# Running sums of a background stream, pinned in program order on VectorE

## The chip, the core and the metric

One Trainium2 chip; the kernel is one program on one of its cores. TensorE (PE in the profile) multiplies matrices, VectorE (DVE) and ScalarE (ACT) work element by element, SyncE (SP) issues nearly all transfers from HBM to the on-chip memory. Each engine takes its own instructions in order and waits on semaphores for the others. The metric is the device time of one execution in microseconds; several runs are given by their median.

## The reference

Two layers of a decoder on 512 tokens of width 2048, float32, batch 1. Each layer is modulated by a condition `c`: shift, scale and gate come from `silu(c) @ w_mod[l] + b_mod[l]`, where `c` is one row, so this is a product of a vector with a matrix.

```python
def reference(x, c, w_mod, ...):
    c_act = jax.nn.silu(c)
    for l in range(DEPTH):                                  # DEPTH = 2
        mod = c_act @ w_mod[l] + b_mod[l]                   # 2048 -> 3 x 2048
        shift, scale, gate = jnp.split(mod, 3, axis=-1)
        h = x * (1.0 + scale[:, None]) + shift[:, None]
        if l < N_A:                                         # layer 0: differential attention, 8 heads
            y = diff_attention(h, a_w_in[l], a_w_out[l], ...)
        else:                                               # layer 1: forgetting attention, 16 heads
            if kv is None:
                kv = shared_kv(x, c_act, kv_w_mod, kv_b_mod, kv_w, kv_b_f)
            y = forgetting_attention(h, b_w_in[l - N_A], b_w_out[l - N_A], *kv)
        x = layer_norm(DN_ALPHA * x + gate[:, None] * y, ln_g[l], ln_b[l])
    return x
```

`shared_kv` has a modulation of its own, `c_act @ kv_w_mod + kv_b_mod` (2048 to 2 x 2048). So six rows of 2048, each a product with a matrix of 2048 x 2048, are needed after the first layer's shift and scale: the gate of layer 0, shift and scale for the shared keys and values, and shift, scale and gate of layer 1.

## The kernel before

**Products.** Every float32 operand is split in a high and a low part (`split`, lines 167 to 169; for weights `WeightStream.step`, lines 93 and 94: ScalarE copies `whi`, VectorE subtracts to get `wlo`). Three matmuls (L173, L174, L175) then make one product. Weights come through `WeightStream`: four staging tiles `wst` filled by SP (L46), three pairs of `whi` and `wlo`. One split covers 256 rows of a weight block of 512 columns and feeds 24 matmuls of 512 columns in a group of four accumulator banks.

**Groups.** `group(job, ...)` runs one block of 512 columns: eight splits, and for each split a burst of six matmuls into each of four PSUM banks, 192 matmuls in all. After each burst it calls `tick`, which takes one step from the list `pieces` (attention steps of the head before: `score`, `turn`, `values`, `store`, evacuations) and up to `bg` steps from the generator `background`. In the last split the `evac` function of the group empties each bank as it ends; the next group reuses the banks.

**Order of work.** A hand-written start (string `START`) computes the first layer's shift and scale and the first products. Then come the groups `kk`, q-k of head 2, v-gate of head 2, then q-k and v-gate of heads 3 to 7, with the attention of the head before in `pieces`. Then four groups of layer 0's output projection (`out_projection`, f = 0 to 3), in the first of which the attention of head 7 runs. Then the shared values and keys (`vj`, `kj`), then layer 1.

**The background stream.** `mod_stream` computes the later modulation rows. For each segment of 512 columns it goes through the 16 row blocks of the matrix: the block is loaded by SP (L368) into `ms`, and VectorE adds it, times the condition's column, to the running sum `macc` (L389 for the first block, L391 for the others). After the last block of a segment `mod_row` splits `macc` (`mhi` on ScalarE, `mlo` on VectorE), sums it over partitions by two matmuls with ones (L411, L412), adds the bias on VectorE (`mrow`, L413) and stores 2 KB (L414). Each sum ends with a `yield`, so one tick with `bg` 1 is one sum. There are two streams:

- The first, 16 segments, 256 sums, in layer 0. An `ms` tile holds two row blocks (512 KB) and there are two such tiles. Ticks take a step only in the q-k groups of heads 3 to 7 (`bg=lambda k: k % 3 > 0`), in the v-gate groups (`k % 4 > 0`) and in the first group of the output projection (`bg` 1). The evacuation of that group's first bank calls `open_n`, which drains what is left of the stream and then folds the shared modulation into columns (`fold`, a transpose at L934).
- The second, 8 segments, 128 sums, in the groups of the shared values and keys; its blocks are single (256 KB), the first 64 in `msk` tiles, the others in `ms`.

**Who sets the order on an engine.** The program is recorded in the order of the Python code, and a scheduler then orders each engine's instructions: by default it may issue an instruction ahead of earlier-written ones if its operands seem ready sooner. Only the start (`tc.manual_schedule`, VectorE) and single instructions pinned by `tc.keep_in_program_order` (one line of `residual_b`) are held. That call records an ordering edge without a wait from the instruction before it on the same engine, so the pinned one isn't issued ahead of that one. Instructions written later may still be issued ahead of it.

Of the kernel before, what the change touches and what calls it, by code (L numbers as in the profile page):

```python
# [13 lines left out]
ALU = mybir.AluOpType  # L14
# [95 lines left out]
def tile_yoco(  # L110
# [24 lines left out]
    V, S, PE, G = nc.vector, nc.scalar, nc.tensor, nc.gpsimd  # L135
# [19 lines left out]
    def acc_bank(name="acc"):  # L155
        return ps.tile([P, 512], F32, name=name, tag="acc", bufs=4)
# [45 lines left out]
    cact = const.tile([P, KT], F32, name="cact")  # L202
# [152 lines left out]
    def mod_stream(segs, new_stage, new_acc, nk, deep=0, new_deep=None):  # L355

        todo = [(i, r) for i in range(len(segs)) for r in range(KT // nk)]
        loaded = {}  # L360
        summed = []

        def load(k):
            i, r = todo[k]
            src, col, _ = segs[i]
            t = new_deep() if k < deep else new_stage()
            rows = src[nk * r * P : nk * (r + 1) * P, col : col + 512]
            nc.sync.dma_start(t, rows.rearrange("(k p) n -> p k n", p=P) if nk > 1 else rows)  # L368
            loaded[k] = t

        def load_upto(k):
            n = len(loads)
            while n < len(todo) and n <= (k + 7 if n < deep else k + 2 // nk):
                load(n)
                loads.append(n)
                n += 1

        loads = []
        load_upto(-1)
        for k, (i, r) in enumerate(todo):  # L380
            load_upto(k)
            if r == 0:
                acc = new_acc()
            t = loaded.pop(k)
            for kk in range(nk):
                kt = nk * r + kk
                w = t[:, kk, :] if nk > 1 else t
                if kt == 0:
                    V.tensor_scalar(acc, w, cact[:, 0:1], None, op0=ALU.mult)  # L389
                else:  # L390
                    V.scalar_tensor_tensor(acc, w, cact[:, kt : kt + 1], acc, op0=ALU.mult, op1=ALU.add)  # L391
                if kt == KT - 1:
                    summed.append(segs[i][2](acc))
                if kt in (1, 5) and summed:
                    if next(summed[0], None) is None:
                        summed.pop()
                yield
        for _ in summed[0]:
            yield
# [22 lines left out]
    with tc.tile_pool(name="start", bufs=2, reuse_waits="tile") as sp, tc.manual_schedule(engines={ET.DVE}):  # L422
# [110 lines left out]
        acc = {}  # L533
# [101 lines left out]
    for dst, src, col, bias, one in (  # L635
# [5 lines left out]
        for f0 in range(0, D, 512):  # L641
            cs = slice(col + f0, col + f0 + 512)
            segs.append((src, col + f0, mod_row(ap, ones_a, dst[:, f0 : f0 + 512], bias[cs], one)))
    background = mod_stream(
        segs,
        lambda: ap.tile([P, 2, 512], F32, name="ms", tag="ms", bufs=2),
# [424 lines left out]
    acc = [acc_bank() for _ in range(TB)]  # L1071
    held = {}
    for i, (half, s) in enumerate(lag):
# [8 lines left out]
        for b in (2 * half, 2 * half + 1):  # L1082
            bs = slice(b * P, (b + 1) * P)
            for kq in range(2):
                kt = 2 * s + kq
# [10 lines left out]
    for dst, col, one in ((mod_dram[1][1:2, :], D, 1.0), (gate_dram[1], 2 * D, 0.0)):  # L1096
        for f0 in range(0, D, 512):
            cs = slice(col + f0, col + f0 + 512)
            segs.append((w_mod[1], col + f0, mod_row(npool, ones_b, dst[:, f0 : f0 + 512], b_mod[1, cs], one)))
    background = mod_stream(  # L1100
        segs,
        lambda: npool.tile([P, 512], F32, name="ms", tag="ms", bufs=3),
# [243 lines left out]
```

## Time and profile before

| what | us |
|---|---|
| median of 3 runs | 2009.19 |
| lowest and highest | 2004.58, 2010.02 |
| the profiled execution | 2010.56 |
| its span, first to last instruction | 2008.7 |
| running sums L389 and L391, VectorE, 384 in all | 281.0 |
| weight splits L94, VectorE, 338 | 403.4 |
| VectorE idle ahead of sums, for their loads | 98.8 |
| SP waiting to issue an `ms` or `msk` load until a sum is done | 143.9 |

The profile gives, for each engine, busy time, share and number of instructions; for each group of instructions line, operation and tiles, and which other engine or transfer ended the wait before it. A line number is one of the kernel as printed above. A matmul of 512 columns is shown with 0.39 us but the next one starts 0.23 us later, since they are pipelined; so a share of 98% for TensorE means that it hardly ever waits, not that it does nothing else. Time that an engine waits matters only where TensorE waits for it in turn.

### The profile page before, as it was taken

How to read it: one execution, taken by the hardware profiler on the slowest of the kernel's cores; microseconds unless marked ns; L12 is line 12 of the kernel's file. 1: busy time of each engine (PE TensorE's matmuls, PEld its weight loads, DVE VectorE, ACT ScalarE, POOL GpSimd, SP SyncE). 2: the span in 40 equal slices, each digit the busy share in tenths (PEclk: the TensorE clock that was granted, in tenths of full speed). 3: DMA queues.
4: the chain of work that ended last, by engine and by line, in shares of the span. 5: the costliest groups of instructions: out<-in, count | busy, mean ns of one | idle time of the engine just before them, and what ended most of it. 6: DMA issues, size and time to landing. Idle time of an engine off the chain costs nothing.

```text
span 2008.7 us, 25012 instructions
## 1 busy us (share of the span) xinstructions
PE 1964.6 (98%) x9115; PEld 1627.1 (81%) x9115; DVE 1335.3 (66%) x2436; ACT 725.6 (36%) x1235; POOL 2.2 (0%) x10
## 2 busy tenths in 40 slices
PE   5999999999999999999999999999999999999996
PEld 4888878888888888788888888888888888888885
DVE  6887865677777777853576666635455555576578
ACT  2432445333333334431263222224343434353232
POOL 0000000000000000000000000000000000000000
PEclk8999999999999999999999999999999999999998
DMA  9994742375757676452346787634323232333664
GB/s 338 348 314 147 237 157 78 111 228 182 226 182 229 191 223 209 161 166 95 118 144 223 234 275 260 224 95 131 100 90 105 95 105 90 104 123 104 215 210 178
DMA packets 263095, 353.79 MB, mean 176 GB/s; under 512 B 18022, under 2 KB 162556, under 8 KB 262204
## 3 DMA queue, kind: packets, MB, share of 16 engines
q1 hardware_dynamic: 260592, 347.99, 53.2%
q10 hardware_dynamic: 2380, 4.21, 0.6%
q8 instruction: 71, 1.16, 0.2%
q14 instruction: 52, 0.43, 0.1%
HBM read 339.47 MB, written 12.66 MB: 175 GB/s over the span
## 4 chain that ended last, share of the span: by engine, by line
PE 87%; DVE 6%; DMA 4%; issue 1%; SPq 1%; ACT 0%; DVEq 0%; ACTq 0%
PE acc L173 25%; PE acc L174 25%; PE acc L175 25%; DMA ms<-in_w_mod_dram 3%; PE sc L173 2%; PE sc L174 2%; PE sc L175 2%; DVE wlo L94 1%; PE o L175 1%; PE o L173 1%; PE o L174 1%; DVE macc L391 1%; PE tr L1203 1%; DMA sms<-in_w_mod_dram 1%; SPq L454 0%
## 5 line engine op out<-in xcount | busy, mean ns | idle before, releaser
L94 DVE TENSOR_TENSOR wlo<-wst,whi 128x1024 fp32r<-128x1024 f32 (+2 forms) x338 | 403.4, 1196 | 278.9 <-ACT whi L93 276.9
L93 ACT CAST whi<-wst 128x1024 fp32r<-128x1024 f32 (+2 forms) x338 | 348.5, 1032 | 640.8 <-PE acc L175 327.5
L173 PE MATMUL acc<-whi,hh 128*128 128x512 f32 x1244 | 488.6, 396 | 1.7 <-DVE sg L680 1.7
L174 PE MATMUL acc<-wlo,hh 128*128 128x512 f32 x1244 | 485.3, 390 | 0.8 <-DVE wlo L94 0.8
L175 PE MATMUL acc<-whi,hl 128*128 128x512 f32 x1244 | 485.0, 390 | 0.0
L173 PE MATMUL acc<-hh,whi 128*128 128x512 f32 x1184 | 470.4, 397 | 0.9 <-DVE part L561 0.5
L174 PE MATMUL acc<-hl,whi 128*128 128x512 f32 x1184 | 462.3, 390 | 0.0
L175 PE MATMUL acc<-hh,wlo 128*128 128x512 f32 x1184 | 462.2, 390 | 0.0
L391 DVE SCALAR_TENSOR_TENSOR macc<-ms,cact,macc 128x512 f32<-128x512 f32 x300 | 224.9, 750 | 86.1 <-DMA ms<-in_w_mod_dram 59.4
L173 PEld LDWEIGHTS acc<-whi,hh 128*128 128x128 f32 x1244 | 234.9, 189 | 49.0 <-PE acc L175 1.4
L175 PEld LDWEIGHTS acc<-whi,hl 128*128 128x128 f32 x1244 | 233.6, 188 | 50.0
L174 PEld LDWEIGHTS acc<-wlo,hh 128*128 128x128 f32 x1244 | 233.8, 188 | 46.7 <-DVE wlo L94 1.2
L175 PEld LDWEIGHTS acc<-hh,wlo 128*128 128x128 f32 x1184 | 222.3, 188 | 48.6
L173 PEld LDWEIGHTS acc<-hh,whi 128*128 128x128 f32 x1184 | 222.6, 188 | 43.5 <-issue 0.9
L174 PEld LDWEIGHTS acc<-hl,whi 128*128 128x128 f32 x1184 | 222.8, 188 | 39.3
L481 DVE SCALAR_TENSOR_TENSOR sacc<-sms,cact,sacc 128x512 f32<-128x512 f32 (+1 forms) x127 | 89.5, 705 | 6.1 <-DMA sms<-in_w_mod_dram 2.4
L710 ACT ACTIVATE e<-e,mn 128x128 f32<-128x128 f32 (+3 forms) x64 | 36.1, 564 | 126.4 <-DVE mn L706 126.2
L1192 ACT ACTIVATE eb<-eb,mnb 128x128 f32<-128x128 f32 (+1 forms) x64 | 36.1, 564 | 95.5 <-DVE mnb L1189 94.4
L1189 DVE CUSTOM_DVE_ANT_0 eb<-sc,biasb 128x128 f32<-128x128 f32 (+1 forms) x64 | 31.4, 490 | 55.4 <-PE sc L175 55.4
L391 DVE SCALAR_TENSOR_TENSOR macc<-msk,cact,macc 128x512 f32<-128x512 f32 x60 | 44.5, 749 | 14.7 <-DMA msk<-in_w_mod_dram 13.6
L1207 DVE TENSOR_TENSOR pTl<-tr,pTh 128x128 fp32r<-128x128 f32 (+1 forms) x64 | 31.2, 487 | 25.2 <-ACT pTh L1206 24.7
L706 DVE CUSTOM_DVE_ANT_0 e<-sc,bias 128x128 f32<-128x128 f32 (+3 forms) x64 | 31.1, 486 | 20.9 <-PE sc L175 20.9
(259 smaller groups left out, 1776.5 us busy)
## 6 DMA issues: line engine op xcount, KB each, us to landing
wst<-in_a_w_in_dram SPq DMA_DIRECT2D x240, 256.0 KB
ms<-in_w_mod_dram SPq DMA_DIRECT2D x64, 512.0 KB
ms<-in_kv_w_mod_dram SPq DMA_DIRECT2D x64, 512.0 KB
wst<-in_kv_w_dram SPq DMA_DIRECT2D x64, 512.0 KB
wst<-in_b_w_in_dram SPq DMA_DIRECT2D x128, 256.0 KB
sms<-in_w_mod_dram SPq DMA_DIRECT2D x56, 512.0 KB
wst<-in_b_w_out_dram SPq DMA_DIRECT2D x48, 512.0 KB
wst<-in_a_w_out_dram SPq DMA_DIRECT2D x32, 512.0 KB
```

What stands on the lines that cost most here:

```text
L93: self.nc.scalar.copy(hi[:, :, :w], st[:, :, :w])
L94: self.nc.vector.tensor_tensor(lo[:, :, :w], st[:, :, :w], hi[:, :, :w].bitcast(F32), op=ALU.subtract)
L173: PE.matmul(dst, lhs[0], rhs[0], start=start, stop=False)
L174: PE.matmul(dst, lhs[0], rhs[1], start=False, stop=False)
L175: PE.matmul(dst, lhs[1], rhs[0], start=False, stop=stop)
L391: V.scalar_tensor_tensor(acc, w, cact[:, kt : kt + 1], acc, op0=ALU.mult, op1=ALU.add)
L481: V.scalar_tensor_tensor(acc, w, sc, acc, op0=ALU.mult, op1=ALU.add)
L706: V.tensor_tensor_reduce(out=e[:, :w], in0=sc[:, :w], in1=st["bias"][:, (3 - i) * P :], scale=-1.0, scalar=3.0e38, op0=ALU.add, op1=ALU.mi ...
L710: S.activation(e[:, :w], e[:, :w], AF.Exp, bias=mn, scale=-1.0, accum_out=rs)
L1189: V.tensor_tensor_reduce(out=e[:, :w], in0=sc[:, :w], in1=bias[:, :w], scale=-1.0, scalar=3.0e38, op0=ALU.add, op1=ALU.min, accum_out=mn)
L1192: S.activation(e[:, :w], e[:, :w], AF.Exp, bias=mn, scale=-1.0, accum_out=rs)
L1207: V.tensor_tensor(pTl[:, 0 : i + 1, ts], src, pTh[:, 0 : i + 1, ts].bitcast(F32), op=ALU.subtract)
```

## The change

```diff
             for kk in range(nk):
                 kt = nk * r + kk
                 w = t[:, kk, :] if nk > 1 else t
+
                 if kt == 0:
-                    V.tensor_scalar(acc, w, cact[:, 0:1], None, op0=ALU.mult)
+                    ins = V.tensor_scalar(acc, w, cact[:, 0:1], None, op0=ALU.mult)
                 else:
-                    V.scalar_tensor_tensor(acc, w, cact[:, kt : kt + 1], acc, op0=ALU.mult, op1=ALU.add)
+                    ins = V.scalar_tensor_tensor(acc, w, cact[:, kt : kt + 1], acc, op0=ALU.mult, op1=ALU.add)
+                tc.keep_in_program_order(ins)
                 if kt == KT - 1:
                     summed.append(segs[i][2](acc))
                 if kt in (1, 5) and summed:
```

Each of the 384 running sums is pinned behind the VectorE instruction that was written just before it. The same instructions run, with the same operands; buffers, loads and ticks are the same. What differs is the place of the sums in VectorE's order, and, where the scheduler follows, the places of the loads on SP and of some matmuls. The numbers of lines behind the change go up by two, so L389, L391, L411, L413 and L934 of the kernel before are L390, L392, L413, L415 and L936 of the changed one.

## Prediction

> **What bounds the kernel now.** I read the shares of busy time first, then TensorE's waits from 180 to 1000 us, then VectorE's work by stage, and last the stretch in which the moved work lands.
>
> ```profile
> PE 1964.6 (98%) x9115; PEld 1627.1 (81%) x9115; DVE 1335.3 (66%) x2436; ACT 725.6 (36%) x1235; POOL 2.2 (0%) x10
> ...
> PE tr L774 <- DVE og L760: 2.7, 3, 1.3
> PE acc L173 <- DVE sg L680: 2.0, 3, 1.0
> PE o L175 <- DVE al L169: 0.6, 1, 0.6
> PE acc L173 <- DVE part L561: 0.5, 1, 0.5
> ```
>
> TensorE is the bound: it idles 44 us of 2008.7. Some 21 us of that lie before 50 us and 17 after the last matmul, and the diff touches neither. Between 180 and 1000 us it idles some 6 us, always for VectorE. So the change can save a few microseconds at most, and it can lose as many as it makes TensorE wait.
>
> ```profile
> 180.00:300.00 120.00, 116.64 (x543) 95.67 (x542) 90.80 (x190) 47.62 (x100) 0.00 (x0) 1.00 0.61 196
> 300.00:400.00 100.00, 99.50 (x484) 82.82 (x483) 59.26 (x149) 45.84 (x98) 0.00 (x0) 1.00 0.29 92
> 400.00:850.00 450.00, 447.95 (x2101) 371.92 (x2100) 343.33 (x679) 167.01 (x330) 0.00 (x0) 1.00 0.65 205
> 850.00:900.00 50.00, 50.00 (x238) 41.15 (x238) 31.23 (x72) 18.71 (x37) 0.00 (x0) 1.00 0.50 156
> ...
> 180.00:280.00 100.00, 34.36 (x47) 0.62 (x1) 1.00 0.66 212
> 280.00:380.00 100.00, 0.28 (x1) 0.00 (x0) 1.00 0.27 87
> 380.00:830.00 450.00, 157.69 (x217) 8.08 (x13) 1.00 0.65 206
> 830.00:900.00 70.00, 4.71 (x7) 1.24 (x2) 1.00 0.46 145
> ```
>
> The first four rows are busy times of PE, PEld, DVE, ACT and POOL, then clock, DMA share and GB/s. The last four are VectorE and ScalarE on the tile `macc` alone. The scheduler has floated 48 running sums (with their splits 47 rows by 280 us) in front of the place where the loop writes them, into 180 to 300 us. There VectorE is busy 91 of 120 us and TensorE misses 3.4 us. The other side is calm: at 850 to 900 us the sums are over, VectorE has 19 us to spare, and TensorE misses nothing.
>
> **What the change moves.** No instruction is added or removed: 384 sums, 512 KB `ms` and 256 KB `msk` loads, 24 rows. I count in weight splits (`wlo`, L94, numbered from 0; four a pair of banks, one per 24 matmuls), because they stand in both programs in the same order. Before: sum 48 lies ahead of split 51, sum 256 (the last of the first stream) ahead of split 139. After: the first sum stands ahead of split 56, the 227th ahead of split 139, the 256th ahead of split 147. This is the loop's own count: 21 ticks in a q-k group and 24 in a v-gate group, 45 a head, 225 in five heads, and the rest in the first group of the output projection.
>
> (1) The early stretch, 180 to 300 us. 48 sums leave (36 us of VectorE at 0.750 us, row L391) and with them 24 loads. TensorE's waits there are 0.5 (`part`), 0.6 (`al`) and 2.2 (`og` at 258 and 275 us), together 3.3 us. Each waits for a chain on VectorE that has sums in it or just ahead. Bounds: 0 if the chains alone are that long, 3.4 (all idle time) if not. I take -3.3, since VectorE falls from 91 to some 55 us of 120 here.
>
> (2) The heads, 330 to 835 us. Sums per head stay the same (before 217 `macc` rows from 380 to 830, splits among them; after 45 a head), only more even: 3, 3, 1, 3 instead of 4, 4, 5, 0. TensorE missed 2 us here, in two evacuations (L680) that keep their sums. 0, from -2 to +3.
>
> (3) The first projection group, 838 to 885 us. It holds the last head's attention and now 29 more sums. Split 139 begins at 838.01 and ends at 839.24; this is where the stretch ends:
>
> ```profile
> 880.93 0.39 PE L411 MATMUL tr<-mhi,ones_a 128*128 128x512 f32 x1
> ...
> 882.87 0.24 PE L934 MATMUL tr<-ident,mrow 32*128 32x32 f32 x1
> ...
> 881.99 0.67 DVE L413 SCALAR_TENSOR_TENSOR mrow<-tr,mrow 1x512 f32<-1x512 f32 x1
> ...
> 883.53 1.28 DVE L899 TENSOR_TENSOR ztmp<-acc,gate 128x512 f32<-128x512 f32 x2
> ...
> 839.24:861.15 21.91, 21.91 (x110) 18.36 (x110) 14.78 (x45) 9.77 (x22) 0.00 (x0) 1.00 0.21 73
> 861.15:883.53 22.38, 22.38 (x110) 18.25 (x109) 10.49 (x27) 9.43 (x20) 0.00 (x0) 1.00 0.58 190
> ```
>
> VectorE does 14.8 + 10.5 = 25.3 us of work in 44.3 us before it evacuates bank 0 (`ztmp`). The 29 sums add 28 x 0.750 + 0.486 = 21.5 us: 46.8 us of work in 44.3. Now the waits. VectorE is in order, a sum waits for its load, and `ms` has two buffers of two sums. The densest run of sums in this trace is the measure:
>
> ```profile
> 710.64 1.54 DVE L391 SCALAR_TENSOR_TENSOR macc<-ms,cact,macc 128x512 f32<-128x512 f32 x2 [1.28 <-DMA ms<-in_w_mod_dram]
> 713.99 1.54 DVE L391 SCALAR_TENSOR_TENSOR macc<-ms,cact,macc 128x512 f32<-128x512 f32 x2 [1.80 <-DMA ms<-in_w_mod_dram]
> ...
> 725.40 1.54 DVE L391 SCALAR_TENSOR_TENSOR macc<-ms,cact,macc 128x512 f32<-128x512 f32 x2 [0.88 <-DMA ms<-in_w_mod_dram]
> ```
>
> From 705.38 to 726.94 it does 14 sums, 1.54 us a sum, while its only other work is four splits; the chain of waits shows 5.6, 3.7 and 4.4 us per load. Splits 140 to 142 get 11 of the sums: 14.8 + 8.2 - 0.7 (an `mlo` that comes later) = 22.3 us of work, against 21.9 us of time, of which 7.1 were waits for scores, exponents and copies. I keep half of these: 26 us, plus 1.5 us for the 1.6 us more work in splits 128 to 139, ends split 142 near 866.7 instead of 861.15. Splits 143 to 147 get the other 18: at 1.54 us, 27.7 us. Their work fits inside: 13.2 for the sums, 4.9 for four splits, 0.7 each for `mlo`, `mrow` and `al`, 2.8 for a norm chain, 1.4 for two `hl`, 24.4 us. So the last sum ends near 894.4, and with ScalarE's copy and the `mlo` (0.6 + 0.7 us, rows L168 and L169) the pair for L411 is ready at 895.8.
>
> What is late next: in the changed program L411, L412 and L934 stand behind all 192 matmuls of the group instead of 18 and 12 earlier, directly ahead of the next group, which begins at 885.21 now. TensorE is in order and waits there. From L411 to the end of the first `ztmp` it now takes 2.9 us without the interposed matmuls; then banks 2 and 3 come 0.9 us late, because six operations of 0.6 us stand between the pairs of evacuations and two bursts last 2.7. Next group: 895.8 + 2.9 + 0.9 = 899.6, against 885.2: +14.4, say +14. The waits inside the attention (L727 and L774, whose inputs come some 2 to 5 us late) are part of these 14, not beside them. Lower bound, no wait at all: 839.2 + 22.3 + 24.4 + 1.3 + 2.9 - 885.2 = +5. Upper, all waits of before kept and loads at 5.6 us throughout: 2.5 at the start, 29.5 and 32 us: +23. The lead of the splits (three buffers, some 11 us) hides none of this, since `ztmp`, L411 and the transposes have no such lead. What follows is light (1.2 us a split of 5.4), so nothing more is lost, and nothing is won back, since TensorE is full.
>
> (4) SP: `ms` loads leave the queue between 180 and 300 us and stand among the weight loads at 840 to 890: 15 loads or 7.9 MB in some 58 us, 136 GB/s more on the 128 there, which is near the 238 GB/s of 704 to 727 us. 0, in the bounds of (3).
>
> (5) The second stream, 128 sums: before in splits 182 to 217, after in 182 to 229, 2 to 3 a split. The fullest splits hold 5.9 us of work for 5.4 us of matmuls, twice, with light ones around. 0; without their lead, +1.
>
> Sum: -3.3 + 14 = +10.7. The profiled execution took 2010.56, the median is 2009.19; on the median, **2020**.
>
> **A rule against it.** The clock is the column before the last two:
>
> ```profile
> 1996.00:1997.00 1.00, 0.00 (x0) 0.95 0.00 0
> 1997.00:1998.00 1.00, 0.00 (x0) 0.50 0.00 0
> ```
>
> The last matmul ends at 1992.6 and the granted clock falls to 0.50 at 1996.9, 4.3 us later; at the start it is 0.50 for 3.1 us of matmuls from 34.26. So a single wait of over 4.3 us at L411 costs half of 3.1, 1.5 us, more. My walk has waits of some 5 us in the attention and 6 to 8 us at L411. [...]
>
> **Rivals.**
> - *The cover holds* (not slower). Place: splits 139 to 147. If scores and loads are early and TensorE's own spare 4 us (`og` ends at 857, L774 is at 861) and the split's lead take up the lateness, only (1) is left: 2005.9. It decides if VectorE's lateness at the first `ztmp` stays under 1.7 us (885.2 - 883.5). For it: loads cost the heads only 41 us over 112 pairs, 0.37 us a pair. Against: the work alone is 2.5 us too much.
> - *Clock gate*, as above, on top: 2021.5.
> - *Heads*: sums pinned among attention steps wait for loads, and a quarter of those 41 us now shows: 2030. Against: the same rate cost 2 us before.
> - *Even or no effect*: gain and loss at their low bounds cancel, or the order hardly matters: 2009. Against: the built order does move, by up to 48 sums.
>
> **Numbers.** Forecast 0.52 (own range 2012 to 2029), clock gate 0.15, cover holds 0.13, heads 0.10, even 0.10. What can be told from no change is 0.3%, 6 us: below 2003.2 or above 2015.2. Faster: half of cover holds, 0.06. Same: the other half, even, and 0.06 of the forecast's low end, 0.23. Slower 0.71. Range 2006 to 2032: down to the cover, up past heads.
>
> **What would show it.** Right: TensorE full from 200 to 300 us; `macc` absent before 320 us and 29 sums between 840 and 900; a wait of several us at L411 (now L413) for `mlo`; the group after it some 10 us later than the early gain alone would put it. Wrong: no TensorE wait from 840 to 900 us, waits on VectorE spread through the heads, or the early waits still there without sums.

## Result, and the profile after

The changed kernel takes 2023.08 us (median of 5 runs, 2021.46 to 2026.01), the kernel before 2007.38 us (median of 5, 2004.58 to 2010.02): 1.0077 times as long, 95% interval 1.0066 to 1.0088, some 15.7 us more (the two profiled executions took 2023.51 and 2010.56). The forecast was 2020, the range 2006 to 2032.

The page of the changed kernel, its shares of busy time first, then TensorE's waits from 180 to 1000 us (engine, line, tile, what it waited for; us in total, times, longest):

```profile
PE 1969.2 (97%) x9115; PEld 1629.4 (81%) x9115; DVE 1338.5 (66%) x2436; ACT 725.8 (36%) x1235; POOL 2.2 (0%) x10
```

```profile
PE tr L413 <- ACT mhi L168: 8.0, 1, 8.0
PE tr L776 <- DVE al L169: 1.9, 1, 1.9
PE acc L173 <- DVE sg L682: 1.6, 2, 1.0
PE acc L173 <- DVE ztmp L901: 1.2, 1, 1.2
PE tr L936 <- DVE mrow L415: 0.8, 1, 0.8
PE tr L776 <- DVE mrow L415: 0.6, 1, 0.6
```

The work is the same (9115 matmuls, 2436 VectorE instructions), the span is 2021.7 instead of 2008.7. The waits of before for `og` have shrunk from 2.7 to 0.5 us, and one wait of 8.0 us has appeared: L413 is the product with ones that closes the last row of the first stream, and it waits for `mhi`, the rounded copy of `macc` that ScalarE makes behind the last running sum.

The stages of the changed kernel (busy us of PE, PEld, DVE, ACT, POOL, then clock, DMA share, GB/s):

```profile
180.00:300.00 120.00, 120.00 (x565) 99.50 (x564) 62.99 (x152) 49.08 (x102) 0.00 (x0) 1.00 0.30 95
...
400.00:850.00 450.00, 447.25 (x2090) 369.92 (x2089) 347.88 (x685) 168.86 (x334) 0.00 (x0) 1.00 0.66 209
850.00:900.00 50.00, 38.25 (x164) 30.50 (x163) 38.24 (x78) 13.49 (x27) 0.00 (x0) 0.84 0.70 221
...
888.00:890.00 2.00, 0.00 (x0) 0.00 (x0) 0.00 (x0) 0.00 (x0) 0.00 (x0) 0.50 1.01 326
896.00:900.00 4.00, 3.72 (x9) 2.94 (x10) 4.00 (x8) 0.00 (x0) 0.00 (x0) 0.50 0.66 116
900.00:902.00 2.00, 2.00 (x7) 1.55 (x6) 2.00 (x4) 0.00 (x0) 0.00 (x0) 0.62 0.84 249
```

and the tile `macc` alone (DVE, ACT, clock, DMA share, GB/s):

```profile
180.00:280.00 100.00, 0.00 (x0) 0.00 (x0) 1.00 0.31 96
280.00:380.00 100.00, 15.10 (x21) 0.62 (x1) 1.00 0.40 124
380.00:830.00 450.00, 157.07 (x217) 7.75 (x13) 1.00 0.65 208
830.00:900.00 70.00, 25.21 (x35) 1.56 (x3) 0.89 0.71 225
```

From 180 to 300 us no sum is left, and TensorE is full (120.00 of 120, before 116.64). From 850 to 900 us it has 38.25 of 50 where it had 50.00, and the granted clock is down (0.84, before 1.00). The 47 `macc` rows of 180 to 280 us are now 20 more at 280 to 380 and 28 more at 830 to 900. In the heads between, the count is 217 as before.

TensorE where the first projection group ends, changed kernel (start, us, then line, operation, tiles; in brackets the idle time before it):

```profile
884.19 0.39 PE L175 MATMUL acc<-whi,hl 128*128 128x512 f32 x1
892.53 0.79 PE L413 MATMUL tr<-mhi,ones_a 128*128 128x512 f32 x1 [7.95 <-ACT mhi L168]
893.25 0.79 PE L414 MATMUL tr<-mlo,ones_a 128*128 128x512 f32 x1
894.82 0.31 PE L936 MATMUL tr<-ident,mrow 32*128 32x32 f32 x1 [0.77 <-DVE mrow L415]
896.28 0.79 PE L173 MATMUL acc<-whi,hh 128*128 128x512 f32 x1 [1.15 <-DVE ztmp L901]
896.88 0.63 PE L174 MATMUL acc<-wlo,hh 128*128 128x512 f32 x1
897.30 0.63 PE L175 MATMUL acc<-whi,hl 128*128 128x512 f32 x1
...
901.56 0.39 PE L173 MATMUL acc<-whi,hh 128*128 128x512 f32 x1
901.78 0.39 PE L174 MATMUL acc<-wlo,hh 128*128 128x512 f32 x1
```

and VectorE, which it waits for:

```profile
879.20 1.54 DVE L392 SCALAR_TENSOR_TENSOR macc<-ms,cact,macc 128x512 f32<-128x512 f32 x2 [0.33 <-DMA ms<-in_w_mod_dram]
...
882.67 1.54 DVE L392 SCALAR_TENSOR_TENSOR macc<-ms,cact,macc 128x512 f32<-128x512 f32 x2 [0.80 <-DMA ms<-in_w_mod_dram]
884.93 1.54 DVE L392 SCALAR_TENSOR_TENSOR macc<-ms,cact,macc 128x512 f32<-128x512 f32 x2 [0.72 <-DMA ms<-in_w_mod_dram]
...
890.28 1.54 DVE L392 SCALAR_TENSOR_TENSOR macc<-ms,cact,macc 128x512 f32<-128x512 f32 x2 [2.68 <-DMA ms<-in_w_mod_dram]
892.51 0.69 DVE L169 TENSOR_TENSOR mlo<-macc,mhi 128x512 fp32r<-128x512 f32 x1 [0.68 <-ACT mhi L168]
894.09 0.68 DVE L415 SCALAR_TENSOR_TENSOR mrow<-tr,mrow 1x512 f32<-1x512 f32 x1 [0.89 <-PE tr L414]
...
895.55 1.28 DVE L901 TENSOR_TENSOR ztmp<-acc,gate 128x512 f32<-128x512 f32 x2
```

TensorE has finished the group (f0) at 884.6 and cannot begin the next (f1) before VectorE empties a bank, from 895.55 on. VectorE is in order and still at the stream: four pairs of sums, each of which waits for its load. The load of the last pair is issued at 884.24, when the pair two before it frees the buffer (882.67 + 1.54), and the pair starts at 890.28. When f1 does start, its matmuls follow each other by 0.43 us and not by 0.23 us until 901.56. That is the clock: 0.50 from 888 on.

From 180 us on the clock was halved once before, inside f0. Behind the wait of 1.9 us for `al` (862.9 us) there are 3.4 us at 0.50, in which TensorE does the work of some 1.7 us (an estimate: half of 3.4):

```profile
860.50:864.00 3.50, 1.62 (x9) 1.06 (x8) 2.42 (x5) 1.24 (x3) 0.00 (x0) 1.00 0.77 257
864.00:867.40 3.40, 3.40 (x16) 3.20 (x15) 1.98 (x3) 1.44 (x3) 0.00 (x0) 0.50 0.93 305
```

To compare all the runs I number TensorE's accumulating matmuls (7392 in every trace) and take the start of each group, that is of its first such matmul; what that one waits for counts in the stretch before. A runs from the start of `kk` to the v-gate group of head 2 (before: 202 to 281 us), B from there to the start of f0 (to 830), C over f0 and f1 (to 929), D from f2 to the start of layer 1 (to 1385). Behind D every kernel takes the same within 1.2 us.

| kernel | median, us | A | B | C | D |
|---|---|---|---|---|---|
| before (its profiled execution took 2010.56) | 2007.38 | 79.33 | 548.12 | 99.87 | 455.96 |
| changed | 2023.08 | 75.61 | 549.84 | 117.23 | 455.92 |
| e1, first sum alone pinned | 2014.59 | 75.61 | 558.46 | 99.33 | 455.93 |
| e2, second stream alone pinned | 2006.62 | 79.84 | 546.62 | 99.23 | 455.95 |
| e3, a tick for every burst | 2022.4 | 75.63 | 568.86 | 97.46 | 456.01 |
| e5, last three segments alone pinned | 2021.1 | 79.23 | 546.07 | 113.63 | 456.01 |
| e6, last segment in second stream | 2009.53 | 75.62 | 549.22 | 100.78 | 455.94 |
| e7, four single buffers | 2012.35 | 75.61 | 546.96 | 107.94 | 456.01 |
| e8, 30 more matmuls | 2024.34 | 75.61 | 549.18 | 117.39 | 456.01 |
| e9, last two segments in second stream | 2006.95 | 75.63 | 549.33 | 98.92 | 456.90 |
| e13, before with four buffers | 2006.88 | 79.14 | 547.11 | 98.89 | 455.92 |
| e14, e9 with four buffers | 2004.24 | 75.62 | 547.03 | 98.03 | 456.99 |
| e16, 34 more matmuls, later | 2017.92 | 75.62 | 548.51 | 112.10 | 455.95 |
| e17, e3 with four buffers | 2004.75 | 75.63 | 550.75 | 97.41 | 455.93 |

Three executions have the first stream ordered by the scheduler as before: before, e2 and e13. Their A is 79.1 to 79.8, and the profiled execution of before is longer than the two others by 1.3 us in B and 0.8 in C. Against the mean of e2 and e13 the changed kernel gains 3.9 us in A, loses 3.0 in B and 18.2 in C: 17.3 us in all, for 15.7 in the medians (13.2 to 17.7 by the interval).

### The profile page after: what moved, and what is told of

It is laid out like the page before. It is cut to its first block, busy times and chain, and to the rows that moved or that the text cites. A ratio compares the mean times of both kernels' runs of the same rounds, so it can differ in the third digit from the quotient of the medians.

```text
span 2021.7 us, 25014 instructions
## 1 busy us (share of the span) xinstructions
PE 1969.2 (97%) x9115; PEld 1629.4 (81%) x9115; DVE 1338.5 (66%) x2436; ACT 725.8 (36%) x1235; POOL 2.2 (0%) x10
## 4 chain that ended last, share of the span: by engine, by line
PE 88%; DVE 5%; DMA 3%; issue 1%; SPq 1%; ACT 1%; DVEq 0%; ACTq 0%
PE acc L173 25%; PE acc L175 25%; PE acc L174 25%; DMA ms<-in_w_mod_dram 2%; PE sc L173 2%; PE sc L174 2%; PE sc L175 2%; PE o L175 1%; PE o L174 1%; PE o L173 1%; DVE macc L392 1%; DVE wlo L94 1%; PE tr L1205 1%; DMA sms<-in_w_mod_dram 1%; DMA ms<-in_kv_w_mod_dram 0%
## 5 line engine op out<-in xcount | busy, mean ns | idle before, releaser
L392 DVE SCALAR_TENSOR_TENSOR macc<-ms,cact,macc 128x512 f32<-128x512 f32 x300 | 224.3, 748 | 43.1 <-DMA ms<-in_kv_w_mod_dram 24.0
L392 DVE SCALAR_TENSOR_TENSOR macc<-msk,cact,macc 128x512 f32<-128x512 f32 x60 | 45.0, 750 | 1.4
```

Source lines behind the costliest of these rows:

```text
L392: ins = V.scalar_tensor_tensor(acc, w, cact[:, kt : kt + 1], acc, op0=ALU.mult, op1=ALU.add)
```

## Experiments

**e2: the second stream alone.** Does any of it come from behind 930 us?

```diff
-                tc.keep_in_program_order(ins)
+                if nk == 1:
+                    tc.keep_in_program_order(ins)
```

> Only the second stream (128 sums, in the shared values and keys) is pinned. Theory: its sums have cover everywhere, 0 plus or minus 1.5 us against before. Rival (the second stream, which now ends 12 splits later, holds up the building of the second layer's input): 3 to 13 us slower.

Measured 2006.62 us, ratio 0.9997 (0.9989 to 1.0006). The second stream may be pinned or not; A to D are within 1.5 us of those of before, and nothing is lost. The change's effect lies in the first stream.

**e5: the last three segments of the first stream alone.** Is C's loss there without any change earlier?

```diff
-                tc.keep_in_program_order(ins)
+                if nk == 2 and i >= 13:
+                    tc.keep_in_program_order(ins)
```

> Only the sums of the last three segments of the first stream (48 of 256) are pinned; the early ones float as before, and 29 sums stand behind split 139 as in the changed kernel. Theory: the late loss without the early gain, 16 to 19 us slower than before (ratio 1.008 to 1.0095), a wait of 7 to 9 us at L413 and the half clock behind it. Rival (each pinned sum among attention steps costs a little): a fifth of the pins, so at most 3 to 4 us slower.

Measured 2021.1 us, ratio 1.0074 (1.0062 to 1.0086). The loss is there, in C alone (113.63, some 14.5 us over e2 and e13), with A and B as before. So late sums make the loss by themselves. The size was below what I expected: the wait for the last sum is 5.8 us, not 7 to 9, and the ratio lies below the 1.008 to 1.0095 of the theory.

**e1: the first sum alone.** It is held behind split 56, and the scheduler may order the other 255 as it likes.

```diff
-                tc.keep_in_program_order(ins)
+                if nk == 2 and k == 0 and kk == 0:
+                    tc.keep_in_program_order(ins)
```

> Only the very first sum of the first stream is pinned, the other 383 may float. In the built order the stream then begins at split 56, catches up by split 90 and ends at split 139 as before. Theory (early stretch gains, late stretch loses): the early gain stays and the late loss is gone: 3 to 5 us faster than before (ratio 0.9975 to 0.9985), TensorE full from 200 to 300 us, no wait at L413 near 885. Rival (holding the stream back overfills the heads that must catch up, splits 57 to 80): not faster than before, waits of TensorE on VectorE between 330 and 450 us.

Measured 2014.59 us, ratio 1.0035 (1.0022 to 1.0048). My theory said a gain, and it fell. A does shrink to 75.61 and C is that of before, but B grows by 11.6 us: the scheduler makes good the 48 sums between 330 and 480 us, and TensorE waits there (2.7 us for `sg`, 2.7 for `q0l`, 1.7 for `mrow`, 1.3 for `og`, 1.2 for `al`); behind the wait for `sg` come 3.4 us at half clock. The 3.9 us of A are not free money: the 48 sums have to go somewhere.

**e3: a tick for every burst in the q-k groups**, so that all 256 sums are done before f0.

```diff
-        group(qk[h], False, evac, bg=lambda k: k % 3 > 0)
+        group(qk[h], False, evac, bg=1)
```

> All sums pinned, but the q-k groups of heads 3 to 7 take a step after every burst (32 a group instead of 21), so that the 256th sum stands ahead of split 133 and the first projection group holds none. Theory (the loss is the 29 sums in that group): late loss gone, early gain kept, 2 to 5 us faster than before. Rival (pinned sums in the heads cost by themselves): the heads get half as many sums again in the q-k groups, so 3 to 10 us slower than before.

Measured 2022.4 us, ratio 1.0075 (1.0061 to 1.0089). The theory fell again: C is free of the loss, but B is 22 us longer. e1 and e3 left two explanations: VectorE has no room in the heads for the work, or the sums stand at the head of its queue and wait for their loads.

**e6: the last segment in the second stream.** 16 sums leave f0.

```diff
+    segs.pop()
     background = mod_stream(
...
-    segs = []
+    segs = [(w_mod[1], D - 512, mod_row(npool, ones_b, mod_dram[1][0:1, D - 512 : D], b_mod[1, D - 512 : D], 0.0))]
```

> All sums pinned as in the changed kernel, but the last segment of the first stream (16 sums, 4 MB of loads) is made the first of the second stream, so that the first stream has 240 sums and only some 13 of them fall into the output projection f0 (838 to 885 us) in place of 35, none into its last fifth. Theory (the changed kernel loses in f0 because 35 sums at 1.54 us each cannot be done while TensorE does its 44 us): VectorE is done in f0 before TensorE, the wait of L413 of 8.0 us and the half clock behind it are gone, the total is some 15 us below the changed kernel, 2006 to 2010, ratio to before 0.999 to 1.001. Rival (the time is lost at the group boundary whatever the number of sums, by the order of TensorE's pieces): it stays near 2020, ratio 1.006 or more. Rival (the second stream has no room for 16 more): f0 gains but the groups of 1000 us and later lose as much, the start of the last stage late by 10 us again.

Measured 2009.53 us, ratio 1.001 (1.0001 to 1.0019). The wait at L413 is 0.3 us instead of 8.0, C is 100.78, D does not notice 16 sums more. So the loss hangs on how many sums are left for f0, not on the order of TensorE's pieces at its end.

**e7: four single buffers.** The same memory and the same sums, in 256 KB blocks three loads ahead, where it was 512 KB and one load ahead.

```diff
-            while n < len(todo) and n <= (k + 7 if n < deep else k + 2 // nk):
+            while n < len(todo) and n <= (k + 7 if n < deep else k + (2 if deep else 3)):
...
-        lambda: ap.tile([P, 2, 512], F32, name="ms", tag="ms", bufs=2),
+        lambda: ap.tile([P, 512], F32, name="ms", tag="ms", bufs=4),
...
-        2,
+        1,
```

> All sums pinned, the same ticks, but the first stream's weights come as 256 KB blocks of one 128 rows into four buffers in place of two buffers of 512 KB (the same memory, three loads ahead). Theory (part of f0's loss is the pace of the loads: VectorE waits 6.2 us for ms there, and a sum takes 1.54 us of which 0.75 us is its work): with a finer grain the waits shrink to 1 to 3 us, the L413 wait by as much, the total 3 to 5 us below the changed kernel, ratio to before 1.005 to 1.006. Rival (the loads are bound by what the DMA moves at 221 GB/s in f0, the grain means nothing): the waits stay, total within 1 us of the changed kernel, 1.0075.

Measured 2012.35 us, ratio 1.0027 (1.0016 to 1.0038): 10.7 us below the changed kernel, twice what the theory said. VectorE's waits for the loads of the sums, 330 to 830 us, changed kernel and then e7 (tile, what it waited for; us, times, longest):

```profile
DVE macc L392 <- DMA ms<-in_kv_w_mod_dram: 24.0, 19, 3.5
...
DVE macc L392 <- DMA ms<-in_w_mod_dram: 9.7, 10, 1.5
```

```profile
DVE macc L392 <- DMA ms<-in_kv_w_mod_dram: 3.4, 5, 1.0
...
DVE macc L392 <- DMA ms<-in_w_mod_dram: 2.0, 5, 0.7
```

The DMA moved the same in both (203 and 205 GB/s from 330 to 830 us); what changes is how early a load may be issued, and how small it is; no run separates the two. B is back at 546.96, C falls by 9.3 us, and the wait at L413 is 3.2 us.

**e17: e3 with the four buffers.** This tells the two explanations of e3 apart.

> All sums pinned, a tick for every burst in the q-k groups too, as in the run that came out at 2022.4 us and lost some 20 us between 300 and 830 us; and now with the four buffers of 256 KB. Theory (the heads are held up by sums that wait for their loads at the head of VectorE's queue, not by the work of the sums): most of the loss in the heads is gone, the total 2004 to 2010, ratio 0.998 to 1.001. Rival (VectorE's work in the q-k groups is itself too much with 24 us more of sums): a loss of 8 us or more stays in the heads, 2013 or above, ratio 1.003 or more.

Measured 2004.75 us, ratio 0.9993 (0.9984 to 1.0002). From 1.0075 to here with not one instruction of VectorE's work less: B falls from 568.86 to 550.75. The same view for e3 and for e17:

```profile
DVE macc L392 <- DMA ms<-in_w_mod_dram: 17.3, 22, 1.9
...
DVE macc L392 <- DMA ms<-in_kv_w_mod_dram: 13.6, 16, 1.6
```

```profile
DVE macc L392 <- DMA ms<-in_w_mod_dram: 8.2, 11, 1.6
...
DVE macc L392 <- DMA ms<-in_kv_w_mod_dram: 5.3, 9, 1.4
```

So in the heads it was the waiting at the head of the queue: VectorE's work there (192.85 us of `macc` in 500 us, e3 194.12) is within 1%. A part of e3's loss is the clock: behind three TensorE waits of 1.8 to 2.2 us it is 0.50 for some 3.4 us each (from 456.5, 521.4 and 664.7 us on), some 5 of the 22 us by half of these times, an estimate. e17 has no such stretch; its longest TensorE wait is 0.9 us. The 3.9 us that B still has over e2 and e13 may be the work; no run separates that.

**e13: the kernel before with four buffers.** Is the grain worth something by itself?

> The kernel before, nothing pinned, with the first stream's weights in four buffers of 256 KB in place of two of 512 KB, as in the four-buffer run of the changed kernel, which came out at 2012.35 us and not at 2023. Theory (the fine grain only cures what pinning made late; before, the sums of the first stream ran early where nothing waited for the loads, and its stall of 4.4 us at 180 to 300 us comes from those early sums): no gain, 2006 to 2009, ratio 0.999 to 1.001. Rival (the grain is worth several us by itself in any order): 2000 to 2004, ratio below 0.998.

Measured 2006.88 us, ratio 1.0002 (0.9994 to 1.0011). Nothing, and A still has its 79.14. Before, the sums wait just as long for their loads (41.2 us from 330 to 830 us; changed kernel 36.6, e13 25.9), yet TensorE pays little for it (B is 548.12 before and 547.11 in e13). The reading that fits is that the scheduler has put the sums where nothing near is urgent, while pinned they wait in front of work that is.

**e9 and e14: the last two segments in the second stream**, which gets more ticks; e14 with the four buffers of e7.

```diff
+    del segs[-2:]
     background = mod_stream(
...
     segs = []
+    for f0 in range(0, D, 512)[-2:]:
+        segs.append((w_mod[1], f0, mod_row(npool, ones_b, mod_dram[1][0:1, f0 : f0 + 512], b_mod[1, f0 : f0 + 512], 0.0)))
...
-        group(vj[g], True, evac_v(g), bg=lambda k: k % 3 > 0)
+        group(vj[g], True, evac_v(g), bg=1)
```

> All sums pinned, the last two segments of the first stream (32 sums) made the first of the second stream, which gets a tick for every burst in its second and third group to have room for them: 224 sums are placed by the ticks of the heads, none falls into f0, 160 are left for the second stream. Theory (pinning gains 4.4 us at 180 to 300 us, costs 1.75 us in the heads and the rest of the loss sits in f0): the early gain stays, f0's loss turns into a gain of up to 3 us as its VectorE has nothing of the stream left, the total 3 to 5 us below before, ratio 0.9975 to 0.9985. Rival (the second stream's groups lose by a tick for every burst what f0 gains, as the heads did with a tick for every burst): 1.002 or above.

> All sums pinned, the last two segments of the first stream moved to the second (which came out at 2006.95 us, 0.9998 of before, with 4.2 us gained up to 300 us and some 2.4 us given back in the heads), and now the four buffers of 256 KB too, with which the changed kernel gave nothing back in the heads. Theory (what the heads and f0 gave back was waiting for loads): the early gain stays to the end, 2003 to 2005, ratio 0.9975 to 0.9987. Rival (the heads gave it back because VectorE has no room, whatever the loads): as without the four buffers, 0.9995 to 1.0005.

e9: 2006.95 us, ratio 0.9998 (0.9989 to 1.0006), short of the gain expected. A keeps its gain, C is 98.92, but B gives 2.5 us back and D 1.0 for 32 sums more. e14: 2004.24 us, ratio 0.9991 (0.9982 to 1.0): a time as expected (the ratio is a little above, since the kernel before came out at 2006.7 in that comparison). B is 547.03 and C 98.03, and one wait is left from 180 to 1000 us:

```profile
PE tr L777 <- DVE og L763: 0.5, 1, 0.5
```

e14 is the best version of the pinned order: 19 us below the changed kernel. Against the kernel before it is 0.1% faster, less than the 0.3% that can be told here.

**e8 and e16: TensorE kept busy**, for the price of the half clock. e8 puts 30 matmuls that nobody reads at the start of `open_n`; e16 puts 34 at the start of f1.

```diff
+            if k == 1 and layer == 0:
+                spare = sc_bank()
+                for _ in range(34):
+                    PE.matmul(spare, Hh[0][:, 0:P], Hh[0], start=True, stop=True)
             last = k == len(jobs) - 1
```

> The changed kernel with 30 more matmuls of ones (128x512, some 6.8 us) put on TensorE ahead of the first instruction of the next projection's opening, where it waits 8.0 us; nothing else uses what they make. Theory (behind the wait TensorE runs some 5.2 us of matmuls at half clock, which costs 2.6 us more than the wait itself): the clock does not fall at 888, the wait of L413 is 1 to 1.5 us, the next group starts some 0 to 0.5 us otherwise but runs at full clock from its first matmul, total 2 to 2.8 us below the changed kernel, ratio to before 1.0062 to 1.0067. Rival (the low clock is a matter of the records or covers only what waits anyway): no gain, 1.0075 or above.

> The changed kernel with 34 more matmuls (128x512, 7.7 us) placed on TensorE behind the last matmul of f0 and ahead of L413, into a score bank that nobody reads (the run with 30 of them put earlier displaced matmuls of f0 into the gap and left a stall of 3.0 us with half clock behind it). Theory (the half clock behind the wait costs 12 matmuls 0.43 us each in place of 0.23 us, 2.4 us): the granted clock stays 1.0 through 884 to 902, f1's matmuls run 0.23 us apart from the first, the start of f2 comes 2 to 2.6 us earlier than in the changed kernel, ratio to before 1.0062 to 1.0068. Rival (VectorE or the weights of f1 are late as well, so that a full clock only waits for them): the start of f2 within 0.7 us of the changed kernel, 1.0073 or above.

e8: 2024.34 us, ratio 1.0088 (1.0074 to 1.0101). It missed its aim. The extra matmuls ran at 880 us, ahead of f0's last ones, and the stall came back behind them (e8, TensorE):

```profile
894.29 0.40 PE L175 MATMUL acc<-whi,hl 128*128 128x512 f32 x1
897.68 0.79 PE L173 MATMUL acc<-whi,hh 128*128 128x512 f32 x1 [3.00 <-DVE ztmp L901]
898.27 0.63 PE L174 MATMUL acc<-wlo,hh 128*128 128x512 f32 x1
```

A wait of 3.00 us is followed by half clock too, here until 900.8; the wait of 2.4 us at L413 in the same run is not (matmuls start some 0.23 us apart from 891.79 on).

e16: 2017.92 us, ratio 1.0061 (1.0049 to 1.0074), 5.2 us below the changed kernel:

```profile
888.96 0.50 PE L413 MATMUL tr<-mhi,ones_a 128*128 128x512 f32 x1 [1.21 <-ACT mhi L168]
...
891.21 1.89 PE L910 MATMUL sc<-hh 128*128 128x512 f32 x7
892.94 0.39 PE L173 MATMUL acc<-whi,hh 128*128 128x512 f32 x1
893.16 0.39 PE L174 MATMUL acc<-wlo,hh 128*128 128x512 f32 x1
893.39 0.39 PE L175 MATMUL acc<-whi,hl 128*128 128x512 f32 x1
```

The clock is 1.00 throughout (850 to 910 us), and f1 runs 0.23 us a matmul from the first. Twelve matmuls took 5.28 us in the changed kernel (896.28 to 901.56) and take 2.72 here, and f1 as a whole 43.5 us instead of 46.1: the half clock behind the wait costs some 2.6 us, and that time is really lost, since nothing else holds f1 up. But C fell by 5.1 us. The other 2.5 lie ahead of f1. VectorE's last sum ended 2.8 us earlier, counted from f0's start (63.9 instead of 66.7), with the same work (53.7 and 53.8 us) and shorter waits: for loads 5.2 us instead of 6.4, for ScalarE's `o` 0.4 instead of 1.5. And e16 lacks the first stretch at half clock: TensorE's wait for `al` is 1.3 us there instead of 1.9, and the clock stays at 1.00 from 864 to 867.4. That may be some 1.7 of the 2.5 us; why a wait ahead of the added matmuls is shorter stays open.

## Why the prediction was right, step by step

**(1) The early stretch, forecast -3.3: right.** All of TensorE's idle time from 180 to 300 us went with the sums. A is 75.61 to 75.63 in ten kernels without early sums and 79.1 to 79.8 in the four with them: 3.5 to 4.2 us (the wait of 0.5 us for `part` in the kernel before lies ahead of `kk` and is not in A). e13 rules out that finer loads alone would have done it. (TensorE's idle time after the last matmul is 16.1 us, not 17; the sum does not use it.)

**(2) The heads, forecast 0 (from -2 to +3): measured +3.0, and +1.7 over the profiled execution of before: the size was off.** The count of sums is the same, as said, and their waits for loads are no longer. What I missed is that a wait costs by what stands behind it. e7 and e14 take the loss away (546.96, 547.03) by taking the waits away.

**(3) The first projection group, forecast +14 (from +5 to +23): right in its mechanism; its size was in part luck, and the clock was left out.** The wait is at L413 and behind it f1 waits for `ztmp`, as forecast. The 29 sums were paced by their loads: VectorE waited 6.4 us for `ms` from 830 to 895 us. From the end of split 139 to the end of the last sum the walk had 55.2 us (839.2 to 894.4), and the changed kernel took 55.6 (836.26 to 891.83). That agreement hides two errors of some 5 us each. Up to the end of split 142 it took 22.7 us where the walk had 27.5: of the 7.1 us of waits of before, half of which I kept, only 1.3 were left, and VectorE was busy for 20.9 us. From there to the last sum it took 32.8 us where the walk had 27.7, a part of it with TensorE at half clock.

f0 as a whole takes 71.1 us in the changed kernel and 56.4 in the profiled execution of before, 14.8 us more where the walk said 14.4. (f1 begins at 885.9 in the kernel before by the count of matmuls, not at 885.2.) What the sum left out is the clock: f1 takes 46.1 us in place of 43.5, and f0 has its own stretch at half clock, some 1.7 us of TensorE's work; how much of the 14.8 us it makes is not shown, since VectorE sets the end of f0. f0 and f1 together are the 17.4 us by which C grew over the profiled execution of before, and 18.2 against e2 and e13.

**(4) SP: right as far as it goes.** The loads and the weights move 221 GB/s together from 850 to 900 us, and the weights are never what TensorE waits for from 180 to 1000 us. But the stream's two buffers were in the end what set half of the size of (3): with four smaller ones 9.3 us of it are gone. I had put that pace in, at 1.54 us a sum, without asking what it would be with another depth.

**(5) The second stream, forecast 0: right**, by e2.

**Sum and rivals.** Forecast +10.7, measured +13.0 between the two profiled executions and +15.7 between the medians; most of the difference of these two is the profiled execution of before, 3.2 us above its kernel's median. *Clock gate* is what happened, with some 2.6 us behind the long wait for the 1.5 I gave it, and had 0.15; my own main case left it out although its walk had a wait of 6 to 8 us at L411 and the trace of before showed a fall after 4.3. Its condition, a single wait of over 4.3 us, was wrong: the stretch at 864 us came behind a wait of 1.9 us. *The cover holds* fails by the wait at L413 and by e5, *heads* in its size (3.0 us where it had 10), though e1 and e3 show that its mechanism is real when more sums go there. *Even* is out.

The two stretches at half clock in the changed kernel last 3.4 us (864.0 to 867.4) and 13.7 us (887.9 to 901.5). The time ahead of a fall was not always idle: TensorE was busy for 1.62 of the 3.50 us ahead of the first fall. The second came 3.3 us after TensorE's last matmul (884.6 to 887.9), and e8's clock falls near 897.4, 2.7 us after its last one. What decides whether a wait of some 2 us is followed by half clock is not shown.

## What to carry to other kernels

VectorE ran in order here, and a sum that waited for its load cost as much as it delayed the most urgent work behind it: in f0 of the changed kernel 2.68 us of such a wait stand ahead of the last pair of sums, and TensorE waits 8.0 us for what follows that pair. Pinning these sums into their written place was safe in the heads only when their loads were issued early enough for that place: three loads of 256 KB ahead did that (B 546.96 us, in e17 550.75) and one of 512 KB did not (549.84, in e3 568.86), in the same memory; whether it is their number or their size is not shown. Count where background work will end, not only where it starts: the sums moved out of a cheap stretch (4 us) landed in the one group whose end nothing covers (18 us). And a TensorE wait of some 2 us can already have a tail at half clock, so put it in the sum with its own term: of eight waits of 1.8 to 2.7 us between 180 and 1000 us in these runs, six were followed by 3.4 us at 0.50 (changed kernel, e1, e5 and three in e3), and two were not (e1 and e8).

## What the runs showed that I had not expected

The kernels' starts differ more than their insides: `kk` begins at 199.20 to 202.68 us in fourteen traces, while A repeats within 0.02 us in the ten without early sums. A difference under some 3 us between two single profiles should be read by stretches, not by spans.

Loads in pieces half as large and three ahead, in the same memory and at nearly the same GB/s (203 and 205, e3 and e17 214 and 218), cut VectorE's waits ahead of the sums from 36.6 to 8.0 us over 500 us, and e3's from 38.3 to 14.5.
